# One reciprocal for the four row blocks of a softmax, and the products with it behind the last exponential

## The chip, the cores and the metric

The kernel runs on one core of one Trainium2 chip, in a single launch. The metric is the device time of that launch in microseconds. The profile shows five engines: PE (matmul, with its weight loads as PEld), DVE (VectorE), ACT (ScalarE), POOL (GpSimd) and SP, which issues the loads of the weights.

## The reference, cut to what matters

Two transformer layers over 512 positions of width 1024, in float32. Each layer is a gated feed-forward block, an attention block and another feed-forward block. The attention of the first layer joins a sparse attention of 8 heads (a compressed, a selected and a window part, mixed by gates) with a dilated attention of 8 heads; that of the second layer is a latent attention of 16 heads. The part that the change touches is the softmax of each of these attentions:

```python
def _probs(scores, mask):
    s = jnp.where(mask, scores.astype(jnp.float32), -MASK_BIG)
    m = jnp.max(s, axis=-1, keepdims=True)
    p = jnp.where(mask, jnp.exp(s - m), 0.0)
    l = jnp.sum(p, axis=-1, keepdims=True)
    l_safe = jnp.where(l > 0, l, 1.0)
    return p / l_safe, (m + jnp.log(l_safe))[..., 0]
```

## The kernel before, in words

Activations are kept transposed, as eight tiles `x0` to `x7` of 128 features by 512 positions. Every matrix product is made three times, from a high and a low part of each operand (`mm3`, lines 211 to 213), and the weights are split into these parts as they arrive (`fetch`, lines 163 and 164). The four feed-forward blocks are `ffn`; between them stand `even` (first layer's attention) and `mla` (second layer's).

**A head.** An attention is a list of jobs, one for a head, or for one of the two masked parts of a sparse head. There are 24 jobs in `even`: 8 dilated ones (`d8` to `d15`, mask `mdil`) and 16 sparse ones (`s0`, `w0` to `s7`, `w7`, mask `mcau`), whose probabilities are also multiplied by a gate. `mla` has 16 jobs (`h0` to `h15`, mask `mcau`). `job` returns three functions for each:

- `soft` goes through four blocks of 128 queries; block `qt` sees 128·(qt+1) keys, so it is 128, 256, 384 or 512 wide. PE makes the scores into a bank `pb` (line 634 in `even`, 211 to 213 in `mla`). DVE adds the mask and takes the row's minimum of the negated scores (line 437; a second small instruction reads the accumulator out). ACT takes the exponential and sums it (line 440, again with an instruction that reads the sum out). DVE inverts the sum (line 441), and POOL multiplies the block by the inverse and by the gate (line 445).
- `trans` has PE turn the ten 128 by 128 blocks of the lower triangle in three groups of four, four and two, each into a bank `pt` (line 454); the first group holds key block 0 of all four query blocks. ACT and DVE write the high and the low part, `pth` and `ptl`, out of the bank (lines 457 and 458). `pth` and `ptl` exist once (`pt_tiles`).
- `pv` multiplies by the values into the bank `pc` (line 465); ACT and DVE then join the two halves into `of` (lines 496 and 497).

**Buffers.** The probabilities of a head are one tile `p` of 1280 columns with two buffers: the first line 437 of a head must wait until the head two before it has been turned. `pb` has two buffers, `pt` three, `pc` one. The small tile `mn` holds a block's minimum, sum and inverse in four columns; `stats` gives it 8 buffers in `even` and 16 in `mla`.

**Order.** `pipe` writes the program out so that `soft` of the next head stands ahead of this head's fill work (projections and output products, listed by hand in `EVEN` and `MLA`), its `trans` and its `pv`. The last nine fills of the heads of `even` are empty but for the very last (`o4`). Each engine works through its own queue in order. The queues are made at build time by a planner that plays the program on a timeline of its own: where an engine is free there, it takes the instruction written earliest among those whose inputs and buffers are ready. So an instruction written later can stand ahead of one written earlier.

Of the kernel before, what the change touches and what calls it, by code (L numbers as in the profile page):

```python
# [3 lines left out]
P = 128  # L4
# [4 lines left out]
F32, F32R = mybir.dt.float32, mybir.dt.float32r  # L9
AF, OP, AX = mybir.ActivationFunctionType, mybir.AluOpType, mybir.AxisListType  # L10
# [14 lines left out]
def raw(ap):  # L25
    return ap.bitcast(F32)
# [54 lines left out]
class Core:  # L81
# [341 lines left out]
    def job(self, sb, scores, mask, PT, o, v, start, stop, gate=None, after=None, factor=None):  # L423


        nc = self.nc
        st = {}

        def soft():
            pt = st["p"] = sb.tile([P, 1280], F32, name="p", bufs=2)  # L430
            for qt in range(4):
                w = (qt + 1) * P
                ps = self.bank("pb")
                scores(qt, ps, max(256, w))
                d = pt[:, P * qt * (qt + 1) // 2:][:, :w]
                mn = self.stats(sb)
                nc.vector.tensor_tensor_reduce(out=d, in0=ps[:, :w], in1=mask[:, (3 - qt) * P:SEQ],
                                               scale=1.0 if factor is None else factor(qt),
                                               scalar=3e38, op0=OP.add, op1=OP.min, accum_out=mn[:, 0:1])
                nc.scalar.activation(d, d, AF.Exp, bias=mn[:, 0:1], scale=-1.0, accum_out=mn[:, 1:2])  # L440
                nc.vector.reciprocal(mn[:, 2:3], mn[:, 1:2])
                r = 1.0
                if gate is not None:
                    r = gate(qt)
                nc.gpsimd.tensor_scalar(d, d, mn[:, 2:3], r, OP.mult, OP.mult)

        def trans():
            pt = st["p"]
            for b0, blocks in ((1, [(0, 0), (1, 0), (2, 0), (3, 0)]), (5, [(1, 1), (2, 1), (3, 1), (3, 3)]),
                               (9, [(2, 2), (3, 2)])):  # L450
                ps = self.bank("pt")
                for i, (qt, kt) in enumerate(blocks):
                    c = P * (qt * (qt + 1) // 2 + kt)
                    nc.tensor.transpose(ps[:, i * P:(i + 1) * P], pt[:, c:c + P], self.ident)  # L454
                n = len(blocks)
                src = ps[:, :n * P].rearrange("p (a b) -> p a b", b=P)
                nc.scalar.activation(PT[0][:, b0:b0 + n, :], src, AF.Copy)
                nc.vector.tensor_tensor(PT[1][:, b0:b0 + n, :], src, raw(PT[0][:, b0:b0 + n, :]), OP.subtract)

        def pv():  # L460
            ps = o()
            for kt, q0, b in ((0, 0, slice(1, 5)), (1, 128, slice(5, 8)), (2, 256, slice(9, 11)),
                              (3, 256, slice(0, 9, 8))):
                for j in range(2):
                    nc.tensor.matmul(ps[:, q0:], v(kt), PT[j][:, b, :], start=start and kt == 0 and j == 0,  # L465
                                     stop=stop and kt == 3 and j == 1)
            if after is not None:
                after(ps)
        return soft, trans, pv

    @staticmethod
    def stats(sb):

        return sb.tile([P, 4], F32, name="mn", bufs=8 if sb.name == "ev" else 16)

    @staticmethod
    def pipe(groups, jobs, do):
# [593 lines left out]
```

## Time and profile before

| what | value |
|---|---|
| median of three runs | 1905.74 us (1904.86 to 1906.49) |
| the profiled execution's own time | 1905.42 us |
| its span, first to last instruction | 1903.7 us |
| PE busy | 1875.1 us (99%) |
| DVE busy | 1359.1 us (71%) |
| ACT busy | 913.5 us (48%) |
| POOL busy | 275.6 us (14%) |

The span is the time between the first and the last instruction of the profiled execution; 1.7 us lie around it. Busy is the time in which an engine had at least one instruction under way. Matmuls overlap and their ends are modelled, so a busy PE may still be fed too slowly. The heads lie between about 405 and 640 us (`even`) and between about 1385 and 1530 us (`mla`).

### The profile page before, as it was taken

The page shows a single profiled execution, that of the slowest core. Times are in us where ns is not written, and L with a number is a line of the kernel's source. Part 1 is how long each engine was busy: PE and PEld are TensorE (multiplying, and loading weights), DVE is VectorE, ACT ScalarE, POOL GpSimd, SP SyncE. Part 2 cuts the span into 40 slices and gives each one's busy share as a digit, 9 for nine tenths or more (in the row PEclk, how much of TensorE's full clock was granted, in tenths as well). Part 3 has the DMA queues.
Part 4 walks back from the last instruction along what each step waited for, and adds up shares of the span by engine and source line. Part 5 has one row for each costly group of instructions (what it writes and reads, how often), then busy time and mean ns, then how long its engine had stood idle before and what let it go on. Part 6 is the DMA issues. An engine that isn't in the chain of part 4 may idle for free. (4 is left out here: it accounts for less than half of the span.)

```text
span 1903.7 us, 28711 instructions
## 1 busy us (share of the span) xinstructions
PE 1875.1 (99%) x11138; PEld 1665.1 (87%) x11138; DVE 1359.1 (71%) x2486; ACT 913.5 (48%) x1633; POOL 275.6 (14%) x291
## 2 busy tenths in 40 slices
PE   8999999999999999999999999999999999999998
PEld 6898998878887789899988998998878878989997
DVE  6974786377888788568846774885399878837862
ACT  6442444347586554334434442443378654424442
POOL 0000000274454400000010000000156320000001
PEclk9999999999999999999999999999999999999999
DMA  4332333322111132333332242333310122332331
GB/s 157 100 111 89 101 92 125 122 88 95 57 46 34 45 100 90 111 100 100 110 96 90 83 120 91 93 107 112 120 43 31 56 81 86 122 100 81 109 111 66
DMA packets 49849, 174.71 MB, mean 92 GB/s; under 512 B 5793, under 2 KB 6049, under 8 KB 49713
## 3 DMA queue, kind: packets, MB, share of 16 engines
q1 hardware_dynamic: 48960, 171.74, 28.9%
q8 instruction: 87, 1.43, 0.3%
q10 hardware_dynamic: 720, 1.08, 0.2%
q14 instruction: 50, 0.40, 0.1%
q0 software_dynamic: 32, 0.07, 0.0%
HBM read 170.76 MB, written 2.10 MB: 91 GB/s over the span
## 5 line engine op out<-in xcount | busy, mean ns | idle before, releaser
L163 ACT ACTIVATE wh<-w 128x1024 fp32r<-128x1024 f32 (+1 forms) x201 | 212.7, 1058 | 381.5 <-issue 127.9
L164 DVE TENSOR_TENSOR wl<-w,wh 128x1024 fp32r<-128x1024 f32 (+1 forms) x201 | 252.8, 1259 | 161.0 <-ACT wh L163 158.2
L234 POOL TENSOR_TENSOR of<-of,t 128x512 f32<-128x512 f32 x36 | 56.6, 1572 | 1310.4 <-issue 888.5
L211 PE MATMUL pa<-xh,wh 128*128 128x512 f32 (+1 forms) x544 | 190.8, 351 | 3.2 <-ACT wh L163 2.6
L213 PE MATMUL pa<-xh,wl 128*128 128x512 f32 (+1 forms) x544 | 189.9, 349 | 0.5 <-DVE wl L164 0.5
L212 PE MATMUL pa<-xl,wh 128*128 128x512 f32 (+1 forms) x544 | 189.6, 349 | 0.0
L183 ACT ACTIVATE wh<-s 128x512 fp32r<-128x512 f32 x224 | 132.7, 622 | 80.4 <-PE pa L212 32.2
L183 ACT ACTIVATE wh<-w 128x512 fp32r<-128x512 f32 x112 | 70.9, 633 | 198.8 <-PE pb L212 95.5
L184 DVE TENSOR_TENSOR wl<-s,wh 128x512 fp32r<-128x512 f32 x224 | 150.3, 687 | 16.2 <-ACT wh L183 15.7
L211 PE MATMUL pb<-T34h,wh 128*128 128x256 f32 (+1 forms) x528 | 157.9, 299 | 0.0
L212 PE MATMUL pb<-T34l,wh 128*128 128x256 f32 (+1 forms) x528 | 157.9, 299 | 0.0
L213 PE MATMUL pb<-T34h,wl 128*128 128x256 f32 (+1 forms) x528 | 157.9, 299 | 0.0
L211 PE MATMUL pc<-fah,wh 128*128 128x512 f32 x352 | 137.1, 389 | 0.0
L213 PE MATMUL pc<-fah,wl 128*128 128x512 f32 x352 | 137.0, 389 | 0.0
L212 PE MATMUL pc<-fal,wh 128*128 128x512 f32 x352 | 137.0, 389 | 0.0
L211 PE MATMUL pt<-fah,wh 128*128 128x512 f32 x352 | 136.9, 389 | 0.0
L212 PE MATMUL pt<-fal,wh 128*128 128x512 f32 x352 | 136.9, 389 | 0.0
L213 PE MATMUL pt<-fah,wl 128*128 128x512 f32 x352 | 136.9, 389 | 0.0
L211 PE MATMUL pt<-xh,wh 128*128 128x256 f32 x448 | 126.8, 283 | 0.0
L212 PE MATMUL pt<-xl,wh 128*128 128x256 f32 x448 | 126.8, 283 | 0.0
L213 PE MATMUL pt<-xh,wl 128*128 128x256 f32 x448 | 126.8, 283 | 0.0
L211 PEld LDWEIGHTS pa<-xh,wh 128*128 128x128 f32 x544 | 103.6, 190 | 17.2 <-ACT wh L163 3.8
(281 smaller groups left out, 5204.4 us busy)
## 6 DMA issues: line engine op xcount, KB each, us to landing
w<-f_g SPq DMA_DIRECT2D x88, 512.0 KB, 3.6
w<-f_u SPq DMA_DIRECT2D x88, 512.0 KB, 3.6
w<-f_d SPq DMA_DIRECT2D x88, 512.0 KB, 3.6
w<-ev_in SPq DMA_DIRECT2D x16, 512.0 KB, 3.7
w<-ev_out SPq DMA_DIRECT2D x8, 512.0 KB, 3.3
w<-mla_out SPq DMA_DIRECT2D x8, 512.0 KB, 3.3
x<-x SPq DMA_DIRECT2D x8, 256.0 KB, 5.8
w<-ev_vb SPq DMA_DIRECT2D x4, 512.0 KB, 3.3
```

Of the source, the lines that this page charges most:

```text
L163: nc.scalar.activation(h[:, :cols], w[:, :cols], AF.Copy)
L164: nc.vector.tensor_tensor(l[:, :cols], w[:, :cols], raw(h[:, :cols]), OP.subtract)
L183: nc.scalar.activation(h[:, c], src, AF.Copy)
L184: nc.vector.tensor_tensor(l[:, c], src, raw(h[:, c]), OP.subtract)
L211: nc.tensor.matmul(out, wh, xh, start=start, stop=False)
L212: nc.tensor.matmul(out, wh, xl, start=False, stop=False)
L213: nc.tensor.matmul(out, wl, xh, start=False, stop=stop)
L234: eng.tensor_tensor(parts[0], parts[0], sq, OP.add)
```

## The change

Within `soft`, the four blocks of a head now share one `mn` tile of 12 columns: the minima in columns 0 to 3, the sums in 4 to 7, the inverses in 8 to 11. One reciprocal of a 128 by 4 operand stands behind the last exponential, and the four products on POOL stand behind it. Before, each block had its own tile, its own reciprocal of a 128 by 1 operand, and its product right behind it. `stats` now has 4 buffers in `even` and 8 in `mla`. Scores, masks, exponentials, products, `trans` and `pv` are the same instructions as before.

```diff
+            mn = self.stats(sb)
+            ds = []
             for qt in range(4):
...
-                mn = self.stats(sb)
+                ds.append(d)
                 nc.vector.tensor_tensor_reduce(out=d, in0=ps[:, :w], in1=mask[:, (3 - qt) * P:SEQ],
                                                scale=1.0 if factor is None else factor(qt),
-                                               scalar=3e38, op0=OP.add, op1=OP.min, accum_out=mn[:, 0:1])
-                nc.scalar.activation(d, d, AF.Exp, bias=mn[:, 0:1], scale=-1.0, accum_out=mn[:, 1:2])
-                nc.vector.reciprocal(mn[:, 2:3], mn[:, 1:2])
-                r = 1.0
-                if gate is not None:
-                    r = gate(qt)
-                nc.gpsimd.tensor_scalar(d, d, mn[:, 2:3], r, OP.mult, OP.mult)
+                                               scalar=3e38, op0=OP.add, op1=OP.min, accum_out=mn[:, qt:qt + 1])
+                nc.scalar.activation(d, d, AF.Exp, bias=mn[:, qt:qt + 1], scale=-1.0,
+                                     accum_out=mn[:, 4 + qt:5 + qt])
+            nc.vector.reciprocal(mn[:, 8:12], mn[:, 4:8])
+            for qt, d in enumerate(ds):
+                r = 1.0 if gate is None else gate(qt)
+                nc.gpsimd.tensor_scalar(d, d, mn[:, 8 + qt:9 + qt], r, OP.mult, OP.mult)
...
-        return sb.tile([P, 4], F32, name="mn", bufs=8 if sb.name == "ev" else 16)
+        return sb.tile([P, 12], F32, name="mn", bufs=4 if sb.name == "ev" else 8)
```

## Rows read from the trace of the kernel before

**Rows 1.** The page: the span, and busy time of PE, DVE and POOL.

```profile
span 1903.7 us, 28711 instructions
...
PE 1875.1 (99%) x11138; PEld 1665.1 (87%) x11138; DVE 1359.1 (71%) x2486; ACT 913.5 (48%) x1633; POOL 275.6 (14%) x291
```

**Rows 2.** Busy time by stretch: both attentions, in us, with counts.

```profile
core 0: us, PE busy (x) PEld busy (x) DVE busy (x) ACT busy (x) POOL busy (x), PEclk, DMA share, GB/s
405.00:590.00 185.00, 179.00 (x1068) 157.59 (x1067) 151.06 (x395) 121.54 (x274) 90.25 (x96) 0.99 0.22 71
590.00:640.00 50.00, 46.65 (x288) 39.97 (x288) 43.10 (x142) 38.84 (x105) 21.33 (x34) 1.00 0.07 22
...
1400.00:1470.00 70.00, 69.03 (x413) 60.76 (x412) 67.22 (x194) 62.75 (x157) 46.61 (x58) 1.00 0.09 31
1470.00:1530.00 60.00, 60.00 (x334) 52.34 (x334) 47.22 (x111) 36.80 (x80) 21.21 (x26) 1.00 0.20 62
```

**Rows 3.** Groups of DVE by shape, 400 to 1530 us: the reciprocals.

```profile
line engine op names shapes xcount | busy us, mean ns | idle before us <-releasers
...
L441 DVE RECIPROCAL mn<-mn 128x1 f32<-128x1 f32 x160 | 23.8, 156 | 9.7 <-ACT p L440 8.9
L728 DVE RECIPROCAL gt<-gt 128x24 f32<-128x24 f32 x4 | 1.2, 303 | 0.1
...
L757 DVE RECIPROCAL st<-st 128x16 f32<-128x16 f32 x2 | 0.5, 253 | 0.1
```

**Rows 4.** Timeline of DVE in a full stretch of `mla`: start, duration in us.

```profile
1420.49 0.35 DVE L437 CUSTOM_DVE_ANT_0 p<-pb,mcau,rcol 128x128 f32<-128x128 f32 x1
1420.77 0.08 DVE L437 DVE_READ_ACCUMULATOR2_ANT mn<- 128x1 f32 x1
1420.77 0.16 DVE L441 RECIPROCAL mn<-mn 128x1 f32<-128x1 f32 x1
1420.84 0.47 DVE L437 CUSTOM_DVE_ANT_0 p<-pb,mcau,rcol 128x256 f32<-128x256 f32 x1
...
1421.49 1.52 DVE L164 TENSOR_TENSOR wl<-w,wh 128x1024 fp32r<-128x1024 f32 x1 [0.17 <-ACT wh L163]
```

**Rows 5.** Where reciprocals stand: DVE time of line 441 alone, by stretch.

```profile
590.00:640.00 50.00, 4.87 (x32) 1.00 0.07 22
1400.00:1470.00 70.00, 6.05 (x42) 1.00 0.09 31
```

**Rows 6.** The page's groups: the products on POOL, without and with the gate.

```profile
L445 POOL TENSOR_SCALAR p<-p,mn 128x128 f32<-128x128 f32 (+1 forms) x96 | 57.2, 603 | 68.3 <-DVE mn L441 66.1 <-PE pb L213 1.2 <-DVE z L700 0.3
...
L445 POOL TENSOR_SCALAR p<-p,mn,gt 128x128 f32<-128x128 f32 (+1 forms) x64 | 43.1, 679 | 57.2 <-DVE mn L441 53.4 <-PE pc L465 2.7 <-PE pb L634 0.3
```

**Rows 7.** Groups of POOL by shape, `even`: the last block's product.

```profile
L445 POOL TENSOR_SCALAR p<-p,mn,gt 128x512 f32<-128x512 f32 x16 | 13.8, 862 | 5.0 <-DVE mn L441 4.6
```

**Rows 8.** Groups of POOL by shape, `mla`: the query's split, the last product.

```profile
L875 POOL TENSOR_TENSOR ql<-t,qh 128x512 fp32r<-128x512 f32 x16 | 22.1, 1384 | 9.4 <-ACT qh L874 9.1
L445 POOL TENSOR_SCALAR p<-p,mn 128x512 f32<-128x512 f32 x16 | 13.2, 824 | 11.6 <-DVE mn L441 11.6
```

**Rows 9.** Timeline of one head (`w6`) near the end of `even`, all engines.

```profile
616.28 0.28 DVE L437 CUSTOM_DVE_ANT_0 p<-pb,mcau 128x128 f32<-128x128 f32 x1
...
620.68 0.72 ACT L440 ACTIVATE p<-p,mn 128x512 f32<-128x512 f32 x1
...
620.98 1.60 POOL L445 TENSOR_SCALAR p<-p,mn,gt 128x384 f32<-128x384 f32 x2 [1.17 <-DVE mn L441]
...
621.53 0.16 DVE L441 RECIPROCAL mn<-mn 128x1 f32<-128x1 f32 x1 [0.65 <-ACT p L440]
...
622.85 0.63 PE L454 MATMUL pt<-ident,p 128*128 128x128 f32 x4 [0.30 <-DVE ptl L458]
...
625.16 0.60 ACT L457 ACTIVATE pth<-pt 128x512 fp32r<-128x512 f32 x1
...
626.02 0.38 PE L454 MATMUL pt<-ident,p 128*128 128x128 f32 x2
...
627.49 0.28 DVE L437 CUSTOM_DVE_ANT_0 p<-pb,mcau 128x128 f32<-128x128 f32 x1
```

**Rows 10.** The products' own view: who waited for line 445 (us, times).

```profile
  PEld pt L454: 0.5, 1
```

**Rows 11.** Timeline of POOL, same stretch as rows 4: a product.

```profile
1421.90 1.68 POOL L445 TENSOR_SCALAR p<-p,mn 128x512 f32<-128x512 f32 x1
```

## The prediction

> **What bounds the kernel now.** I read the page first: PE is busy 99% of the span, DVE 71%, POOL 14% [rows 1]. Over the whole run PE is the bound, and an instruction taken from DVE or POOL is worth nothing where PE has work in hand. The change touches only the attentions, so the next view is busy time by stretch [rows 2]. There are four kinds of stretch. From 405 to 590 us the heads of the first layer run beside projections: PE 179.0 of 185 us, DVE 151.1 (82%). From 590 to 640 us the last heads run with no fill work: PE 46.65 of 50, DVE 43.1 (86%). From 1400 to 1470 us, in the second layer, DVE is full: 67.2 of 70 us (96%), beside PE at 69.0. From 1470 to 1530 us PE is busy all 60 us and DVE 47.2. So DVE has a say in the second and third stretch, 120 us together; in the other two its work is mostly covered by PE. Since PE's ends are modelled, its idle time in rows 2 (3.35 us and 0.97 us there) is a lower bound of what a faster supply could win.
>
> The third view is one head near the end of the first layer [rows 9]. Its first masked minimum starts at 616.28, the last exponential at 620.68, the last reciprocal at 621.53 after DVE had waited 0.65 us for ACT, and the last two products end at 620.98 + 1.60 = 622.58. Then come the first four transposes at 622.85, the ACT copy out of a bank at 625.16, the last two transposes at 626.02, and, 1.1 us after these end, the first minimum of the head two later at 627.49, which needs the same `p` buffer. The reader is to see two loops: over `p` (two heads deep) and over `pth`/`ptl` (one head deep). The four transposes ended at 622.85 + 0.63 = 623.48 and the copy came 1.7 us later: this head waited for the second loop, not for its products.
>
> **What is removed.** 120 of 160 reciprocals, at 156 ns each [rows 3]. Taken at full duration that is 18.7 us of DVE. But the timeline shows what one costs in a full queue: a reciprocal starts at 1420.77 together with the accumulator read ahead of it, and the next line 437 starts at 1420.84 [rows 4]. It holds DVE for 0.07 us there and overlaps the rest. All 120 at 0.07 us are 8.4 us. In the two stretches where DVE counts there are 32 + 42 = 74 reciprocals [rows 5]; three in four go, 55, so 55 × 0.07 = 3.9 us, against 55 × 0.156 = 8.6 us at full duration. In the stretch at 96% DVE's share passes best, at 86% only in part; I let half of it reach the end: −1.9 us. The bounds are 0 (PE covers it all) and −8.6 us.
>
> Here the Trainium skill has a rule of its own: "VectorE: DVE Perf Modes", section "The DRAIN you can't avoid", has the next DVE instruction start only when the pipe has emptied, and advises keeping the count of instructions low. By it each removed reciprocal would give back its whole duration, the −8.6 us above instead of −3.9 us. The two overlapping starts in rows 4 speak against that here.
>
> DVE also stood idle 9.7 us ahead of the 160 reciprocals, 8.9 of them until an exponential ended [rows 3]. The one that stays waits for the last exponential, as the fourth did (0.65 us in rows 9); what the first three waited goes. I give no credit for it, as DVE's other waits can grow into the gap; three quarters, 7.3 us, is its upper bound and belongs to the faster rival.
>
> **What is added.** The 40 reciprocals that stay are 4 wide. The 16 and 24 wide ones take 253 and 303 ns [rows 3]; from 156 ns at width 1 that is (253 − 156)/15 = 6.5 ns a column, so some 175 ns at width 4: 40 × 0.02 = 0.8 us of DVE over the whole run, 0.2 us in each full stretch at most. I leave it out.
>
> **What is moved.** The first three products of a head now stand behind the last exponential. Before, they mostly ran while later blocks were still in work; now POOL runs four in a row. With the gate the four take 4 × 0.679 = 2.72 us and the last one 0.862 [rows 6, 7], so the last product ends 1.85 us later. Without it: 4 × 0.603 = 2.41, less 0.824 [rows 6, 8], 1.6 us later. No DMA is moved and nothing passes a load on SP. On POOL, the first product waits for the reciprocal; behind it stand the query's split (1384 ns each, [rows 8]), the rotary products and the low halves of the outputs. On DVE, the reciprocal's wait holds up the next head's minima and the `ptl` subtractions.
>
> What is late next are the transposes. Today they never wait for a product: 0.5 us, once, in the whole run [rows 10]. For the head of rows 9, products end 1.85 us later, at about 624.4; its first group then ends near 625.3 instead of 623.48, and the copy at 625.16 would move by some 0.2 us, as the 1.7 us of slack take the rest. That is a gated head; an ungated one loses less. For the 8 heads of the stretch without fill work (32 reciprocals, rows 5) I take 8 × 0.2 = +1.6 us. The bounds: 0, and, if the `p` loop carries it all, 1.85/2 for each head as two buffers are in flight, 8 × 0.92 = +7.4 us. In the second layer the planner has other work for PE and DVE while products are late; I take 0 there. If that cover is gone it costs up to 1.6/2 = 0.8 us for each of some 10 heads in the full stretch, +8 us.
>
> The shared tile has 4 and 8 buffers for a whole head each, against 2 and 4 heads' worth before; `p` with two buffers binds earlier, so this costs nothing.
>
> **The sum.** The profiled execution took 1905.42 us, 1.7 us more than its span, and lies 0.3 us below the median of the runs. 1905.42 − 1.9 + 1.6 = 1905.1 us; I say 1905.
>
> **The rivals.** A measurement of this kernel can tell a change from none from about 0.2%, 3.8 us.
>
> (a) *Faster: DVE was the bound, and the waits ahead of reciprocals were on the path.* For it: 96% in rows 2, and 9.7 us of idle time in rows 3. Full-duration relief in the two stretches, −8.6 us, or −3.9 us with half of the 7.3 us of waits, −7.5 us; with +1.6 us for late products −6 to −7: about 1899 us. Against: rows 4, and that PE is busy 69 of 70 us beside it. Chance 0.30.
>
> (b) *Slower: the `p` loop closes later.* Place: the transposes of the last heads of the first layer. Price: 0.92 us a head, +7.4 − 1.9 = +5.5 us: 1911 us. It decides when the slack between transposes and copy is below the 1.85 us by more than half a microsecond a head. For it: rows 9 show the next user of the buffer 1.1 us behind the last transposes, so there is little to spare in that loop. Against: the 1.7 us in the same rows. Chance 0.19.
>
> (c) *Slower: POOL becomes a queue.* POOL is busy 46.6 of 70 us in the full stretch [rows 2]. A product of 0.7 to 0.8 us took 1.68 us beside a weight subtraction on DVE, which itself took 1.52 us [rows 4, 11]. If each block of four meets one such, its last product is about 1 us later still, and the query's split behind it too: 18 heads × 0.5 us, less 1.9: +7 us, 1912 us. The Trainium skill, "GPSIMD Engine Reference", section "Key points", says that POOL and DVE share SBUF interfaces and contend when DVE has two inputs there; that would make such blocks common, and rows 11 agree for one of them. Chance 0.07.
>
> (d) *The edit does not do what it says:* the four blocks' columns of one tile might be ordered as one, so that each minimum waits for the exponential before it: three waits of up to 0.72 us [rows 9], some 2 us a head, or +20 us and more over the heads of the two stretches. Rows 4 speak against it: two blocks already share the tile `p`, and the second minimum starts at 1420.84 as soon as DVE is free. Chance 0.01.
>
> **How the numbers follow.** My forecast, DVE's relief and the late products nearly cancelling within 3.8 us either way, has 0.43. Faster is (a), 0.30; slower is (b), (c) and (d), 0.27. The range takes in (a) at 1899 and (b) at 1911 and leaves out the ends beyond both: 1899 to 1911. The forecast's own range is 1902 to 1909.
>
> **What would show it.** Line 441 with 40 instructions of 160 to 190 ns. Four products in a row on POOL for nearly every head. DVE some 7 to 9 us less busy in all. Transposes that follow the last product, still with hardly a wait on PE. If the first minimum of a head in the last stretch moves by much more than 0.2 us a head, (b) holds; if `ql` and the scores in the second layer come later, (c); if PE's count of matmuls in the full stretch rises clearly, (a). My number would be wrong above all if the planner, with other ready times, lays the fill work differently around the heads: then both attentions shift by more than the terms that I priced.

## The result, and the profile after

The changed kernel is slower: 1918.49 us (median of 6 runs, 1917.09 to 1919.5) against 1906.12 us of the kernel before (6 runs), a ratio of 1.0064 with a 95% interval of 1.0051 to 1.0076. That is +12.4 us, between 9.7 and 14.5. The forecast was 1905 us with a range up to 1911 us.

First the page of the changed kernel, which answers to [rows 1].

```profile
span 1916.9 us, 28568 instructions
...
PE 1883.2 (98%) x11138; PEld 1668.1 (87%) x11138; DVE 1349.7 (70%) x2366; ACT 912.8 (48%) x1633; POOL 268.7 (14%) x291
```

DVE has 120 instructions and 9.4 us less, PE has the same 11138 matmuls, and the span is 13.2 us longer. Busy time by stretch, with the columns of [rows 2]:

```profile
405.00:590.00 185.00, 177.48 (x1055) 156.44 (x1053) 143.54 (x341) 119.86 (x272) 88.80 (x95) 0.98 0.22 68
590.00:640.00 50.00, 45.14 (x260) 37.37 (x261) 39.40 (x113) 35.74 (x95) 20.22 (x32) 1.00 0.11 32
1400.00:1470.00 70.00, 66.35 (x371) 57.38 (x372) 63.62 (x152) 57.58 (x142) 38.23 (x50) 0.95 0.10 31
1470.00:1530.00 60.00, 59.62 (x344) 51.87 (x343) 46.73 (x109) 42.94 (x99) 24.55 (x36) 1.00 0.17 53
```

In every one of the four stretches both PE and DVE are less busy than before. DVE got its relief. The counts of matmuls tell little here: the stretches are fixed in time and the second layer's heads begin 9 us later, so fewer fall between 1400 and 1470 us (371 for 413) and more behind that (344 for 334). The view of the reciprocals' own line answers to [rows 3] (count, duration in ns as minimum, median and maximum):

```profile
L444 DVE RECIPROCAL mn<-mn x40: 157/174/179, 421.4 to 1527.0; 128x4 f32<-128x4 f32 x40
its engine sat idle before it (us, times) until:
  ACT p L442: 7.2, 11
who waited for it (us, times):
  POOL p L447: 112.9, 26
```

And those who waited for the products, as in [rows 10]:

```profile
who waited for it (us, times):
  POOL ql L878: 1.3, 1
  PEld pt L456: 0.5, 2
```

So PE hardly ever stands and waits for a product on the chip, 0.5 us in the whole run as before. The loss does not show as a wait at the place that was edited. It shows in the order. Here is the end of the first layer's attention, from the timelines of DVE, ACT, POOL and PE: the head of [rows 9] (`w6`), then `s7` and `w7`.

```profile
623.30 0.27 DVE L439 CUSTOM_DVE_ANT_0 p<-pb,mcau 128x128 f32<-128x128 f32 x1
...
628.49 0.72 ACT L442 ACTIVATE p<-p,mn 128x512 f32<-128x512 f32 x1
...
629.85 0.17 DVE L444 RECIPROCAL mn<-mn 128x4 f32<-128x4 f32 x1
...
630.23 2.37 POOL L447 TENSOR_SCALAR p<-p,mn,gt 128x128 f32<-128x128 f32 x4 [0.37 <-DVE mn L444]
633.14 2.37 POOL L447 TENSOR_SCALAR p<-p,mn,gt 128x128 f32<-128x128 f32 x4 [0.53 <-DVE mn L444]
...
634.90 0.60 PE L456 MATMUL pt<-ident,p 128*128 128x128 f32 x4
...
636.85 0.28 DVE L439 CUSTOM_DVE_ANT_0 p<-pb,mcau 128x128 f32<-128x128 f32 x1
...
639.46 0.39 PE L213 MATMUL pa<-oh,wl 128*128 128x512 f32 x1
639.68 0.33 PE L637 MATMUL pb<-kh,q 128*128 128x384 f32 x1
...
640.90 0.60 PE L456 MATMUL pt<-ident,p 128*128 128x128 f32 x4
...
653.21 0.39 PE L668 MATMUL pc<-cl,vc 128*128 128x512 f32 x1
655.66 0.73 PE L211 MATMUL pa<-oh,wh 128*128 128x512 f32 x2 [2.06 <-ACT oh L650]
```

Three things are to be seen. The four products of a head now stand in a row behind its last exponential (2.37 us). `s7`'s end at 633.14 + 2.37 = 635.51 us, but its transposes run at 640.90: between them PE works through output products (the `pa<-oh` up to 639.46) and only then makes the last scores of `w7`. And when the last head is done at 653.6 us, PE has to wait 2.06 us for the split of the last pair: the output products that ran behind the last head before are used up. The same 24 us behind the last head's last product, before and after:

```profile
643.80:667.80 24.00, 23.35 (x103) 17.73 (x102) 17.95 (x22) 13.10 (x20) 11.61 (x7) 1.00 0.22 66
```

```profile
653.10:677.10 24.00, 19.87 (x90) 14.41 (x88) 16.07 (x19) 11.58 (x19) 10.14 (x7) 1.00 0.14 44
```

PE does 3.5 us less there, yet the way from this point to the second layer's heads takes as long as before (750.5 us before, 750.3 after).

**Where the 12.4 us are.** I took four marks from each profile: the end of the last matmul of heads 15 and 23 of `even` (counted from 0; `w4`, behind which the eight heads without fill work begin, and `w7`), and the first minimum and the last matmul of the heads of `mla`. These are the last matmuls of heads 15 and 23 before, and that of head 15 after (that of head 23 is the one at 653.21 us above):

```profile
601.47 0.39 PE L665 MATMUL pc<-cl,vc 128*128 128x512 f32 x1
...
643.90 0.40 PE L665 MATMUL pc<-cl,vc 128*128 128x512 f32 x1
```

```profile
605.21 0.40 PE L668 MATMUL pc<-cl,vc 128*128 128x512 f32 x1
```

From head 15 to head 23 it is 42.4 us before and 48.0 us after (+5.6). Between these marks PE makes 72 output products after the change and 55 before; the 17 more, at some 0.23 us each, are most of the 5.6 us. They are work brought forward, and it becomes a loss where it is missing, in the 24 us behind the last head. `mla`, from first minimum to last matmul, before and after:

```profile
1394.80:1524.40 129.60, 128.62 (x744) 113.22 (x744) 115.32 (x312) 100.44 (x242) 67.37 (x85) 0.99 0.13 42
```

```profile
1403.90:1537.80 133.90, 132.35 (x744) 113.96 (x744) 112.34 (x264) 101.86 (x242) 61.71 (x85) 0.98 0.13 40
```

That is 129.7 us and 133.9 us (+4.2). The first 16 heads are read from several profiles, as single ones scatter: six with the order of before end head 15 at 601.9 to 605.6 us (mean 603.7), seven with the order of after at 604.4 to 607.5 us (mean 606.3), so +2.5. Much of the scatter is the granted clock. From the first minimum of `even` to this mark, profiles at a clock of 0.98 take 193.8 to 194.1 us in the order of before (three) and 196.8 to 197.0 us in that of after (two); at 0.97 it is 196.5 us (two) and 197.7 to 199.0 us (four). In all +12.3 us.

### The profile page after: what moved, and what is told of

It is laid out like the page before. It is cut to its first block, busy times and chain, and to the rows that moved or that the text cites. A ratio compares the mean times of both kernels' runs of the same rounds, so it can differ in the third digit from the quotient of the medians.

```text
span 1916.9 us, 28568 instructions
## 1 busy us (share of the span) xinstructions
PE 1883.2 (98%) x11138; PEld 1668.1 (87%) x11138; DVE 1349.7 (70%) x2366; ACT 912.8 (48%) x1633; POOL 268.7 (14%) x291
## 5 line engine op out<-in xcount | busy, mean ns | idle before, releaser
L183 ACT ACTIVATE wh<-s 128x512 fp32r<-128x512 f32 x224 | 132.5, 621 | 80.1 <-PE pa L212 32.7
```

What stands on the lines that cost most here:

```text
L183: nc.scalar.activation(h[:, c], src, AF.Copy)
```

## The experiments

Theory 1 was that the last product of a head is later, and the heads' chain with it. Theory 2: the batched reciprocal itself, or DVE's new queue. Theory 3: the shared tile. Later a fourth took their place: the planner deals a new order to everything behind the edit, and the order of before was a good one. Times below are medians beside the kernel before on the same chip (1905.95 to 1906.08 us), with the ratio and its interval.

**The parts by themselves.** First the written order without the batch, and the shared tile without the late products.

```diff
# late_only: products written behind the last exponential, one reciprocal each
+                late.append((d, mn))
+            for qt, (d, mn) in enumerate(late):
...
                 nc.gpsimd.tensor_scalar(d, d, mn[:, 2:3], r, OP.mult, OP.mult)
# tile_only: one mn of 12 columns, reciprocal and product in the loop
+                nc.vector.reciprocal(mn[:, 8 + qt:9 + qt], mn[:, 4 + qt:5 + qt])
...
```

> The kernel before with its own tile and reciprocal for each block, but the four products of a head behind its last exponential. Theory 1 (late products: the last product of a head ends 1.6 to 1.85 us later and the transposes behind it move): the whole loss is here, 1916 to 1922 us, since the 120 reciprocals that the change saves are still paid. Theory 2 (the single 4 wide reciprocal that waits for the last exponential stalls DVE): about 1906 us. Theory 3 (the shared tile or its buffers): about 1906 us.

> The changed kernel's shared 12 column tile and its buffer counts, but a reciprocal and a product for each block right behind its exponential. Theories 1 and 2: the queues come out as in the kernel before, 1905 to 1907 us. Theory 3: 1915 us or more.

`late_only` 1906.96 us, ratio 1.0002 (0.9993 to 1.0011); `tile_only` 1906.04 us, 1.0002 (0.9992 to 1.0011). In both, every engine's instructions stand in the very order of the kernel before. For the tile that settles it: it costs nothing, and the columns are not ordered as one. For `late_only` it means that the test missed its aim. A product that is written later still runs as soon as its own reciprocal is there, so nothing was late. It is the single reciprocal that makes the products late.

**Half the batch, and lateness alone.**

```diff
# three_one: one reciprocal behind the third exponential, one behind the last
+                if qt in (2, 3):
+                    q0 = 0 if qt == 2 else 3
+                    nc.vector.reciprocal(mn[:, 8 + q0:9 + qt], mn[:, 4 + q0:5 + qt])
...
# pad2: the kernel before, two products by 1.0 ahead of block 3's own (pad1: one)
+                for _ in range(2 if qt == 3 else 0):
+                    nc.gpsimd.tensor_scalar(d, d, 1.0, 1.0, OP.mult, OP.mult)
```

> The changed kernel with two reciprocals a head: one 3 wide behind the third exponential with its three products, one behind the last with the last product. 80 reciprocals fewer than before, and the three early products can run under the last exponential. Theory 1: the last product is hardly later than before, 1902 to 1909 us. Theory 2: half of the waits are back, but two of three stalls stay joined: 1910 to 1915 us. If any other order of the products costs, whatever its lateness, 1912 us or more.

> The kernel before with the last block of each head multiplied by 1 twice on POOL, in place, between its exponential and its product: the last product of a head ends about 1.3 us later, DVE keeps its 160 reciprocals, and POOL gains 80 products (some 56 us). Theory 1 (the last product's lateness costs, through the order that the planner makes with it): 1913 to 1920 us. Theory 2 (the joined reciprocal and its wait on DVE): 1905 to 1908 us. Theory 4 (any other ready time deals the queues anew, by chance a bad hand in the changed kernel): anything from 1900 to 1918 us, with no relation to the lateness.

> The kernel before with one more product by 1.0 on POOL ahead of block 3's own, so that the last product of each head ends about 0.75 us later instead of 1.5 us; 40 instructions are added on POOL and nothing else. Lateness as a dose (the loss grows with how late the last product is): half of the 15 us that two such products cost, 1911 to 1915 us. Order as dealt (a new list order costs what it happens to cost, whatever the dose): no fixed relation, anything from 1905 to 1922, and other stretches than with two. Slack (up to a point late products are free): 1905 to 1908.

`three_one` 1908.18 us, 1.0010 (1.0001 to 1.0019); `pad2` 1920.99 us, 1.0076 (1.0061 to 1.0091); `pad1` 1916.89 us, 1.0060 (1.0044 to 1.0077). `pad2` keeps all 160 reciprocals and loses as much as the change, in the same places (49.0 us for the last eight heads, 133.7 us for `mla`): the batch as such is not needed for a loss of this size, and theory 2 is not either. But `pad1`, with one padding product where `pad2` has two, costs +10.9 us where half of 15 was expected, and `three_one`, in which the last product of the last eight heads comes as late as in `pad1` (1.85 and 1.90 us, means of the eight, from the end of the read-out of the last exponential's sum to the end of the last product; lateness is counted like this throughout), costs 2.2 us. The loss is no smooth function of lateness, as far as these two compare: `three_one` also has 80 reciprocals less on DVE.

**The loop over `p`, and POOL relieved.**

```diff
# after_p3ml
-            pt = st["p"] = sb.tile([P, 1280], F32, name="p", bufs=2)
+            pt = st["p"] = sb.tile([P, 1280], F32, name="p", bufs=3 if sb.name == "ml" else 2)
# two_engines
+                eng = nc.gpsimd if qt < 2 else nc.vector
+                eng.tensor_scalar(d, d, mn[:, 8 + qt:9 + qt], r, OP.mult, OP.mult)
```

> The changed kernel with three buffers of p in the second layer's attention in place of two (the first layer's has no room for it). If the p loop closing later carries the loss of the second layer (some 4 of the 13 us between the two profiles), 1912 to 1915 us, with the second layer's heads as long as before the change. If the loss there comes from elsewhere (fill work placed differently, DVE order), 1918 us as the change.

> The changed kernel with the products of the two wide blocks on DVE and those of the two narrow ones on POOL, so that a head's four products are done about 1 us behind the reciprocal, not 2.4 to 2.7. DVE gains 80 products, POOL loses them. Theory 1: most of the loss is gone, 1904 to 1911 us, though DVE works more. Theory 2 or a DVE bound: as slow as the change or slower, 1918 to 1930 us.

`after_p3ml` 1918.76 us, 1.0066 (1.0051 to 1.0081): a third buffer takes nothing off `mla` (134.4 us), so rival (b)'s loop is not what costs there, as far as one kernel whose order changes too can tell. In `even` a third buffer does not fit and was not tried. `two_engines` 1923.63 us, 1.0092 (1.0077 to 1.0107), against the 1904 to 1911 of theory 1: moving two products to DVE shortens the row on POOL and is still slower. The time lies where the expectation had put a bound on DVE: DVE is busy 67.72 of the 70 us from 1400 to 1470 there, more than in [rows 2], and `mla` takes 136.7 us. More work on DVE thus goes with a loss there, which does not say that less of it is a gain.

**DVE's relief by itself.**

```diff
# no_recip: the kernel before without its reciprocals
-                nc.vector.reciprocal(mn[:, 2:3], mn[:, 1:2])
-                nc.gpsimd.tensor_scalar(d, d, mn[:, 2:3], r, OP.mult, OP.mult)
+                nc.gpsimd.tensor_scalar(d, d, mn[:, 1:2], r, OP.mult, OP.mult)
```

> The kernel before without the 160 reciprocals: POOL multiplies each block by its raw sum, so the values differ, and the products come some 0.2 to 0.3 us earlier, none later. It is the relief of DVE alone, and a third larger than in the change. Rival (a) of the prediction, DVE as the bound: 8 to 11 us less, 1895 to 1898. The prediction's own term, half of 0.07 us for each reciprocal in the two stretches: about 2.6 us less, 1903. Relief worth nothing: 1905 to 1907.

1908.60 us, 1.0013 (1.0004 to 1.0022): slower by 2.6 us, although work was only taken away and the last products come earlier (0.88 us behind the last exponential in the last eight heads, where it was 1.34). Its page:

```profile
PE 1878.1 (98%) x11138; PEld 1667.4 (87%) x11138; DVE 1349.5 (71%) x2326; ACT 911.8 (48%) x1633; POOL 272.2 (14%) x291
```

DVE's busy time fell from 1359.1 to 1349.5 us, 0.06 us for each of the 160 reciprocals of 156 ns: [rows 4] again, over the whole run. By the rule that the prediction took from the Trainium skill, "VectorE: DVE Perf Modes", section "The DRAIN you can't avoid", each would have given back its full duration, 25 us; this run does not bear that out. The same section adds that a next instruction that is not held back starts earlier, and with this the 0.06 us agree. Rival (a), which priced 6 to 7 us of gain, did not come with this relief either. The last eight heads took 44.7 us and `mla` 132.7 us, both longer than before; the first 16 heads took 191.8 us, 2 us less than the profiles of the old order at the same clock of 0.98. So the relief, or the earlier products, did gain something in one place and lost more in two others. The run speaks for the fourth theory: an edit that only takes work away still lost in part of the first attention and in the second.

**One layer at a time.**

```diff
# even_only: head < 24; tail_keep: not 16 <= head < 24; mla_only: head >= 24
+            one = head < 24
...
+                if not one:
+                    nc.vector.reciprocal(mn[:, 8 + qt:9 + qt], mn[:, 4 + qt:5 + qt])
+                    r = 1.0 if gate is None else gate(qt)
+                    nc.gpsimd.tensor_scalar(d, d, mn[:, 8 + qt:9 + qt], r, OP.mult, OP.mult)
+            if one:
...
```

> The change in the first layer's 24 heads alone; the second layer's heads keep a reciprocal and a product for each block. From the two profiles some 9 of the 13 us were lost by the end of the first layer: 1912 to 1916 us if the losses of the two layers add. If the second layer's loss only follows from how the first ends, 1917 to 1919 us; 1906 to 1910 us if it was all in the second.

> The change in all heads but the last eight of the first layer (those with no fill work), which keep a reciprocal and a product for each block. If these eight carry the loss of the first layer (theory 1: there a head's own chain sets the end), 1909 to 1912 us: what is left is the second layer's. If the loss is spread over all heads, 1915 to 1917 us.

> The change in the second layer's 16 heads alone; the first layer's heads invert and multiply block by block as before. If the losses of the layers add up, the second layer's attention takes 133 to 135 us, the first layer's stretch from head 15 to head 23 42.4 us, and the time is 3.5 to 5 us above the kernel before, 1909.5 to 1911. If the second layer's loss needs the first layer's (it is planned behind it), 1905.5 to 1908.

`even_only` 1916.39 us, 1.0047 (1.0031 to 1.0064); `mla_only` 1909.43 us, 1.0022 (1.0013 to 1.0032). They lose 10.3 and 3.4 us, 13.7 together, which is the change's 12.4 within what the runs can tell: the layers' losses are separate. `even_only` runs `mla` in the order of the kernel before, `mla_only` in that of the changed one, matmul for matmul. From the first minimum to the last product of `mla`, `even_only` first:

```profile
1405.90:1535.70 129.80, 128.86 (x744) 113.44 (x744) 115.37 (x312) 100.19 (x242) 67.09 (x85) 0.99 0.13 42
```

```profile
1395.70:1528.20 132.50, 131.01 (x744) 112.76 (x744) 112.24 (x264) 101.89 (x242) 61.66 (x85) 0.99 0.13 41
```

At the same granted clock of 0.99 the changed order costs 2.7 us. PE is busy for 2.2 us more with the same 744 matmuls, and its idle time grew by 0.6 us only. Their ends are modelled, so a busy share near 99% does not say that PE loses nothing.

`tail_keep` missed its expectation: it leaves the last eight heads as they were, and they take 42.4 us again, but it runs at 1917.10 us, 1.0055 (1.0040 to 1.0070). In its profile head 15 ends at 608.7 us, and `mla` takes 134.7 us in yet another order. Most of the late end of head 15 is no work of a new order, for up to 601.8 us PE's queue is that of the changed kernel; the first 16 heads take 200.1 us at a clock of 0.97, where that kernel's order takes 197.7 to 199.0 us at 0.97 and 197.0 at 0.98. All four executions of `tail_keep` were granted 0.992 over the span, the six of the changed kernel 0.993 to 0.996, so a part of its time is the clock's.

**The last eight heads with the fill work out of the way.** A pair, the old and the changed softmax, in which the output products `o4` to `o7` may not run before the last head is done.

```diff
-     ... "", "", "", "", "", "", "", "", "o4"]),
-    ([], ["o5 o6 o7"]),
+     ... "", "", "", "", "", "", "", "", ""]),
+    ([], ["o4 o5 o6 o7"]),
...
+                if u in ("o4", "o5", "o6", "o7"):
+                    with self.tc.issue_after(C["end"].ins):
+                        return self.out_proj(oh, EV_PARTS, "ev_out", int(n))
```

> The kernel before, with the last four chunks of output products of the first layer (o4 to o7) ordered behind the last head's last product, so that none of them fills gaps among the last eight heads; the stretch from the end of head 15 to the end of head 23 is then the heads' own chain. It is the partner of the next kernel. By every theory slower than before, since about 16 products of 0.69 us lose their cover: 8 to 20 us, 1914 to 1926; the stretch is 42 us or less, as nothing stands in the heads' way.

> The changed kernel with the same order of the output products as its partner. If late products lengthen the heads' own chain (the loop over the two p buffers), the stretch from head 15 to head 23 stays 5 to 6 us longer than its partner's, and the time 12 to 13 us. If the chain lengthens only by the predicted 0.2 us a head, and the rest of the 5.6 us is output products laid into its way, the stretch is longer by 1 to 2.5 us, and the time by 7 to 9 us (second layer and first part of the first as in the change).

The last matmuls of heads 15 and 23 (line 665, and 668 in the changed kernel) in the first and in the second:

```profile
605.82 0.39 PE L665 MATMUL pc<-cl,vc 128*128 128x512 f32 x1
...
639.84 0.40 PE L665 MATMUL pc<-cl,vc 128*128 128x512 f32 x1
```

```profile
607.06 0.39 PE L668 MATMUL pc<-cl,vc 128*128 128x512 f32 x1
...
643.36 0.40 PE L668 MATMUL pc<-cl,vc 128*128 128x512 f32 x1
```

That is 34.0 us and 36.3 us: left to themselves, the heads' chain is 2.3 us longer with the late products, 0.29 us a head. Of the 5.6 us, the other 3.3 us come with the output products, laid between the heads in another order and in greater number (this is the difference of the two pairs, not a measurement by itself). The times are 1914.36 us, 1.0047 (1.0032 to 1.0062), and 1920.38 us, 1.0072 (1.0057 to 1.0087); the pair is 6.0 us apart, under the 7 to 9 us expected.

The reason for that is the find of this pair. `before_pin` has the old softmax, and its products in `mla` come as early as before (1.88 us behind the last exponential; 2.07 before; 3.33 in the changed kernel). Yet:

```profile
1402.90:1537.50 134.60, 131.42 (x744) 113.48 (x744) 114.99 (x312) 100.56 (x242) 63.49 (x85) 0.99 0.12 41
```

134.6 us, 5 us more than before, at the same clock. (The profile is of this kernel's slowest execution, 1918.43 us; its low clock, 0.97, lies in the first 16 heads.) Pinning four chunks in the first layer had put other instructions in 550 of the 741 places of PE's queue in `mla` (563 in the changed kernel). A new order alone can cost all that the change costs in this layer. `after_pin`, whose `mla` stands matmul for matmul in the order of the changed kernel, takes 133.6 us there, 1 us less than its partner with the early products.

**New orders without an edit.** Two pairs in which two units of `mla`'s fill work change places, so that the order is dealt anew there and only there. In C, query 10 is computed with the next part of the query weights, not its own.

```diff
# swapC
-     ... "Q10 W3", "Q12", ...
+     ... "W3 Q10", "Q12", ...
# swapG
-     ... "V2 K5 Q14", ...
+     ... "K5 V2 Q14", ...
```

> The kernel before with two units of the second layer's fill work, W3 and Q10, written in the other order; the softmax of the heads is untouched and no product is late. If the second layer's loss is that of a favourable order of instructions, lost by any new deal, its attention (first masked minimum to the last head's last product, 129.7 us before) takes 132 to 135 us here too, and the time is 2 to 5 us above the kernel before, 1908 to 1911. If late products are needed for the loss, it stays at 129.5 to 130.5 us and the time at 1905 to 1907.

> The changed kernel with the same two units written in the other order. Favourable order lost: the second layer's attention takes anything from 130 to 136 us, with no fixed distance from its partner. Late products: 133 to 135 us, some 4 us more than its partner.

> The kernel before with another two units of the second layer's fill work, V2 and K5, written in the other order; softmax untouched. Favourable order lost: 132 to 135 us for the second layer's attention, 1908 to 1911 us in all. Late products needed: 129.5 to 130.5 us, 1905 to 1907 us.

> The changed kernel with V2 and K5 written in the other order. Favourable order lost: anything from 130 to 136 us, no fixed distance from its partner. Late products: 133 to 135 us, some 4 us more than its partner.

With the old softmax: C 1908.08 us, 1.0014 (1.0004 to 1.0023), `mla` 131.7 us; G 1906.39 us, 1.0004 (0.9995 to 1.0013), `mla` 130.1 us. With the changed one: C 1920.22 us, 1.0081 (1.0064 to 1.0097), 134.4 us; G 1918.97 us, 1.0074 (1.0059 to 1.0089), 132.5 us. So a swap of two units moved the old kernel's `mla` by 2.0 us in one case and 0.4 us in the other, less than the 132 to 135 us that I expected of both; G came out where I had put it if late products are needed for the loss (129.5 to 130.5 us), and its 0.4 us is within the 129.5 to 129.9 us that four profiles of one order show. Orders with the old softmax now stand at 129.7, 130.1, 131.7 and 134.6 us, those with the changed one at 132.5 to 134.7 us. The two groups overlap, but no order with late products was as good as 130. Against its partner the changed softmax takes 2.7 us more in C (at a clock of 0.98 against 0.99), 2.3 in G, 2.7 without a swap, and 1 us less in the pinned pair.

**The cover given back.**

```diff
# after_cover: the changed kernel
+                if u == "o6":
+                    with self.tc.issue_after(C["end"].ins):
+                        return self.out_proj(oh, EV_PARTS, "ev_out", 6)
```

> The changed kernel with one chunk of output products of the first layer, o6 (8 products of 0.69 us, 5.5 us), ordered behind the last head's last product, so that it can't run among the last heads and is left as cover for the split of the last pair. If the 5.6 us of the last eight heads are cover used too early, the stretch from head 15 to head 23 falls from 48.0 to 42.5 to 44.5 us, the idle time of 2.1 us behind the last head goes, and the time falls by 2 to 4 us, to 1914.5 to 1916.5. If the chain of the late products sets it, the stretch stays above 46 us and the time at 1918 or more.

1918.52 us, 1.0066 (1.0051 to 1.0081): no gain. The 2.06 us of waiting behind the last head are gone, and the last eight heads take 44.9 us in place of 48.0, but 1.6 us of that come back behind them, since the 5.5 us of `o6` (an estimate: 8 products of 0.69 us) stand there now, and `mla`, dealt anew (444 of 741 places differ from the changed kernel's), took 134.6 us in its profile. Giving back the cover of this one chunk is thus worth 1.5 us up to the second layer, and it does not repair the change.

## Why the prediction was wrong

The mechanism of the moved products was named, and its size in the last eight heads was of the right order; what failed is the sum, which had terms only for the instructions that the diff touches and put the fill work around them at nothing.

| step of the prediction | predicted | shown |
|---|---|---|
| DVE, 40 reciprocals | 160 to 190 ns each | 174 ns (median) |
| DVE less busy | 7 to 9 us | 9.4 us |
| what DVE's relief brings | −1.9 us | no gain in all: `no_recip`, +2.6 us with 9.6 us less of DVE |
| last product later, last eight heads | 1.85 us | 1.50 us (from 1.34 to 2.84, means) |
| late products, last eight heads | +1.6 us | +2.3 us, the pinned pair |
| the same heads, output products in another order | 0 | +3.3 us, the rest of 5.6 |
| second layer: late products and the order that comes with them | 0 | +2.7 us, `mla_only` against `even_only` |
| first 16 heads | 0 | +2.5 us, means of six and seven profiles |
| shared tile | 0 | 0, `tile_only` |

The four losses make 10.8 us of the 12.4; the rest is inside the interval, and part of it may be the granted clock, below.

**What is removed.** "In the stretch at 96% DVE's share passes best": it did not show in the sum. Less work on DVE changes when the planner sees it free, and with that the order. In `no_recip` the relief and the new order together gained some 2 us in the first 16 heads and lost more behind them; what the relief would be worth in the order of before, no run shows.

**What is moved** is the step that failed. 0.2 us a head was read from the slack of one head, and the pinned pair measured 0.29. But I wrote "In the second layer the planner has other work for PE and DVE while products are late; I take 0 there", and counted that other work as cover. It is cover only if it fills time in which PE would have stood idle otherwise. At the end of the first layer, which I had priced as a stretch without such work, it was work that already had a place: 17 output products were laid in earlier, stood in the heads' way (the 5.4 us between `s7`'s products and its transposes in the timeline above, most of them filled with output products) and were missing behind them. In the second layer 2.7 us were measured where I took 0; which part of them the late products cost and which part the order, no run shows.

**The rivals.** (a) is contradicted by `no_recip`: the relief alone, in the order that the planner makes with it, shortens nothing in all. (b), the `p` loop, gave the right sign at 1911 us, but is not shown to carry more than the 2.3 us of the last eight heads, and `after_p3ml` speaks against it in the second layer. (c), POOL's queue, did not come as priced: `ql` waited once for a product, 1.3 us in the whole run, and in the second layer the products of the last block became shorter:

```profile
L447 POOL TENSOR_SCALAR p<-p,mn 128x512 f32<-128x512 f32 x16 | 11.2, 697 | 0.0
```

697 ns where [rows 8] have 824; with the gate it was 948 for 862 in [rows 7]. Yet the longest wait of PE in `mla` looks like (c) in another place. Two weight subtractions on DVE stand beside the four products and a query's split on POOL, and all are slow: the two take 3.98 us (one took 1.32 us on average in this attention before), the split 2.27 us (1.37). The minimum of the third block comes behind them, and PE waits for it:

```profile
1431.63 3.98 DVE L164 TENSOR_TENSOR wl<-w,wh 128x1024 fp32r<-128x1024 f32 x2
...
1432.26 2.27 POOL L878 TENSOR_TENSOR ql<-t,qh 128x512 fp32r<-128x512 f32 x1
...
1435.53 0.61 DVE L439 CUSTOM_DVE_ANT_0 p<-pb,mcau,rcol 128x384 f32<-128x384 f32 x1
...
1436.29 0.36 PE L211 MATMUL pb<-kh,qh 128*128 128x256 f32 x1 [1.05 <-DVE mn L439]
```

Summed over `mla` it is little: the 11 weight subtractions take 15.0 us in place of 14.5, the 14 splits 20.2 in place of 19.2. The rule that (c) leant on, in the Trainium skill's "GPSIMD Engine Reference", section "Key points", was not tested here by itself. (d) is refuted by `tile_only`. The sentence that the prediction put last, that the planner may lay the fill work differently around the heads, is what happened; it had been given no price. The order of before is the shortest that any run found for `mla`, so a new deal could hardly have been a gain there.

**What stays open.** Whether late products cost anything of their own in the second layer: 2.7 us lie inside the 5 us by which orders with the old softmax differ, and too few orders were tried to tell a difference of the means. No run kept the old order with late products, which would tell the two apart. Why the first 16 heads lose 2.5 us was not followed up, and what makes the old order good was not found either. And no version here beats the kernel before; `three_one`, the nearest, is level with it to slightly slower.

## What to carry to other kernels

Where a planner or a list deals the order of the queues, price an edit twice: the instructions it touches, and a new deal for everything behind it; a control that deals anew without the edit (two fill units swapped, some work pinned) shows how much that is, here 0.4 to 5 us in an attention of 130 us. To see the chain of a stage by itself, pin the fill work out of its way in both kernels and compare the pair. Batching small operations to spare an engine also delays whoever used the first results: a busy share of 96% on DVE was no reason to do it, as 9.6 us less of it brought no shorter time.

## What the runs showed of the hardware

The granted clock of PE falls for short times in the attentions, most often where one begins, not always at the same place nor as often. Windows of 10 us, before and after:

```profile
1390.00:1400.00 10.00, 6.57 (x30) 5.89 (x30) 8.51 (x19) 5.75 (x14) 3.38 (x4) 0.83 0.00 0
```

```profile
1400.00:1410.00 10.00, 7.46 (x27) 6.58 (x28) 7.22 (x16) 4.55 (x13) 1.69 (x1) 0.66 0.00 1
```

The clock has two levels, 1.2 and 2.4 GHz: at 0.83 a third of the 10 us is at the lower one, at 0.66 two thirds. In both windows PE had been partly idle (busy 6.57 and 7.46 of 10 us). Other profiles show such falls near 415 and 585 us too. What a fall costs can be read where the order is the same: `mla` in the changed order took 132.5 us at a mean clock of 0.99 (`mla_only`) and 133.9 us at 0.98, 1.4 us more. A single profile can't be compared with another to better than that, so the losses in the table are taken from the last eight heads, where the clock was 1.00 in the kernel before and the changed one, from means, or at the same clock.

A reciprocal of 128 by 4 takes 174 ns where one of 128 by 1 takes 156 [rows 3], the 175 ns that were interpolated. In `three_one` those of 128 by 3 took 168 ns.
